# Grouped-query heads: the mean square of each query from TensorE transposes and ScalarE row sums

## The chip, the core and the metric

The kernel runs on one core of a Trainium2 chip. A core has TensorE (PE in the profile, with its weight loads as PEld), VectorE (DVE), ScalarE (ACT), GpSimd (POOL), a queue of its own for transfers (SP), and two on-chip memories: SBUF, and PSUM, which has eight banks and to which TensorE writes its results. Each engine takes its instructions strictly in the order in which the built program lists them, and waits at one until the semaphores that it names have been reached. The metric is the device time of one execution in microseconds (us).

## The reference, cut to what matters

The program is one step of a backbone with two trunk layers and a SwiGLU feed-forward after each. The second layer attends with eight query heads over two key heads, and each query is RMS-normed over its 128 features before it is rotated:

```python
q = rms_norm(q.reshape(b, L, GQA_HEADS, GQA_HEAD_DIM), q_norm)   # x * rsqrt(mean(x*x) + eps) * g
...
q = apply_rope(q, cos, sin)
...
s = jnp.einsum('bqkgd,bskd->bkgqs', qi, k) * scale
p = jax.nn.softmax(s, axis=-1)
```

There are 640 tokens: 512 latent tokens and 128 prompt tokens, in five blocks of 128. The factor rsqrt(mean(q*q) + eps) is one number for each query token, so it can be left out of q and multiplied into the scores of that token's row, inside the exponential of the softmax. Both kernels do that.

## The kernel before, in words

Activations lie with features on the 128 partitions and tokens along the free dimension. Every product is taken in three passes of a split operand (a high part, and a low part that holds the rest): high by high, high by low, low by high. The change touches the grouped-query layer alone.

**A head's queries.** `gqa_q(h)` makes eight pieces, q0 to q7. Pieces q0 to q3 are 24 matmuls that accumulate the first half of the tokens (320 columns) in one bank of PSUM, called `gq`; q4 to q7 do the second half in another. At the end of a half, `done` (L1824) copies the bank to SBUF on ScalarE (L1825, tile `gqc`), squares it on ScalarE (L1826, `gsq`), rotates it on VectorE (`rope`, L1729 to L1732, tile `gqr`) and splits it in high and low (`gqh` on ScalarE, L1829; `gql` on VectorE, L1830).

**The row factor.** `rstd` (L1833) multiplies the squares, as the stationary operand, with two columns of ones: five matmuls in full fp32, each of which the profile records twice, put the sum of squares of each token on that token's partition (tile `gr`). ScalarE turns the five columns into exp(-0.5 ln(mean + eps)), tile `rq` (L1837, L1838).

**Scores and softmax.** `gqa_scores` makes pieces s0 to s4, one for each block of 128 queries. Six matmuls write a score tile `gs` of 128 queries by 640 keys (s4, the prompt: 128 by 128) into one of two pairs of banks. VectorE takes the row maximum (`gn`, L1854), multiplies it with `rq` (`gb`, L1864), and ScalarE writes the exponential with its row sum (`gp`, L1865); an ACTIVATION_READ_ACCUMULATOR that follows fetches the sum. GpSimd divides by the sum (L393). For the first block this second half stands in the order as a piece of its own, x0, behind r.

**Values.** `values` transposes the weights, four 128x128 transposes a block (pieces t0 to t4, tile `gt`), splits them in `gts_h` on ScalarE (L401) and `gts_l` on VectorE (L402), and multiplies them with the values (pieces v0 to v4, tile `go`; the prompt's are pt, pv, `gtp`, `gop`). `oG` (L1893, L1894) is the head's output in SBUF.

**The order.** The loop at the end runs one pass for each head h. A pass has the scores of head h, the queries of head h + 1 and the values of head h - 1, and issues them to TensorE in the order of the string `GQA_ORDER`. The order of the other engines is chosen by a scheduler when the program is built.

**Banks.** Tiles `gq`, `gr`, `gt`, `go`, `gtp` and `gop` come from one pool, `psp`, tag "m", of four banks. A new tile takes a bank that an earlier one has given up, and its first matmul waits for the last reader of that earlier tile. `go` holds its bank from v0 to the end of v4. The score pairs take the four other banks (tag "s", two pairs).

**SBUF.** Tag "t" has three tiles of 128x640, tag "u" seven of 128x320.

Of the kernel before, what the change touches and what calls it, by code (L numbers as in the profile page):

```python
# [11 lines left out]
F32 = mybir.dt.float32  # L12
F32R = mybir.dt.float32r
AF = mybir.ActivationFunctionType
# [4 lines left out]
P = 128  # L19
# [5 lines left out]
HT = T // 2  # L25
# [26 lines left out]
def body(ctx, tc, xT, vecs, crow, wm0, wm0g1, wm0g, wm1, wA, wNV, wNA, wMK, wMV, wOA, wGQ, wGK, wGV, wOC,  # L52
# [3 lines left out]
    V, S, G = nc.vector, nc.scalar, nc.gpsimd  # L56
# [18 lines left out]
    tp = ctx.enter_context(tc.tile_pool(name="tp", bufs=4))  # L75
# [5 lines left out]
    def open_y(**tags):  # L81
        if ypool:
            ypool["stack"].close()
        ypool["stack"] = ExitStack()
        ypool["n"] = ypool.get("n", 0) + 1
        ypool["pool"] = ypool["stack"].enter_context(tc.tile_pool(name=f"psy{ypool['n']}", bufs=1, space=PSUM))
        ypool["tags"] = tags

    def bank(name, kind="m"):
        if kind == "m":  # L90
            return psp.tile([P, 512], F32, tag="m", bufs=4, name=name)
        return ypool["pool"].tile([P, 512], F32, tag=kind, bufs=ypool["tags"][kind], name=name)
# [10 lines left out]
    def tmp(name):  # L103
        return tp.tile([P, T], F32, tag="t", bufs=3, name=name)

    def f(ap):
        return ap.bitcast(F32)
# [7 lines left out]
    def run(pieces):  # L115

        for piece in pieces:
            with tc.issue_after(PE.last.ins):
                piece()

    def sequence(order, pieces):

        left = dict(pieces)
        run([left.pop(name) for name in order.split() if name in left])
        assert not left, list(left)

    def named(prefix, pieces):
        return {f"{prefix}{i}": piece for i, piece in enumerate(pieces)}
# [6 lines left out]
    ones = main.tile([P, P], F32, name="ones")  # L135
    V.memset(ones, 1.0)
    eps = main.tile([P, 1], F32, name="eps")
# [11 lines left out]
    def vcol(i):  # L149
        return vec[:, i:i + 1]  # L150
# [17 lines left out]
    def unit(src, n, name, lo="v", pool=None, bufs=3):  # L168

        raw = load(src, n, name + "r")  # L170
        t = (pool or wp).tile([P, 2, 1024], F32R, tag="w", bufs=bufs, name=name)
        hi, lw = t[:, 0, :n], t[:, 1, :n]
        S.activation(hi, raw, AF.Copy)
        (V if lo == "v" else G).tensor_tensor(lw, raw, f(hi), ALU.subtract)
        return hi, lw

    def after(inst, fn):
        if inst is None:
            return fn()
        with tc.issue_after(inst.ins):  # L180
            return fn()
# [223 lines left out]
    def tr(out, in_):  # L405
        PE.transpose(out, in_, ident)
# [72 lines left out]
    def pieces_of(ps_name, bk, whl, hh, hl, ks, c0, c1, done, w0=0, step=2):  # L479

        box = {}

        def piece(j0, j1):
            def run():
                if j0 == 0:
                    box["ps"] = bk(ps_name)
                wh, wl = whl()
                proj(box["ps"], wh, wl, hh, hl, ks[j0:j1], c0, c1, first=j0 == 0, last=j1 == len(ks), w0=w0 + j0)
                if j1 == len(ks):
                    done(box["ps"])  # L490
            return run
        return [piece(j, min(j + step, len(ks))) for j in range(0, len(ks), step)]
# [4 lines left out]
    def lazy(fn):  # L497
        box = []

        def get():  # L500
            if not box:
                box.append(fn())
            return box[0]
        return get
# [128 lines left out]
    for kk in range(4):  # L633
# [3 lines left out]
        for j in range(2):  # L637
            k = 2 * kk + j
            a, b = wh[:, 512 * j:512 * (j + 1)], wl[:, 512 * j:512 * (j + 1)]
            for i in range(5):  # L640
                c0, c1 = P * i, P * i + P
# [264 lines left out]
    for h in range(8):  # L906
        p, r = divmod(h, 2)
# [9 lines left out]
        pieces = named("s", sc)  # L917
# [60 lines left out]
    def mla_scores(h, pts, beside):  # L978
        r = h % 2
        ll = tiny.tile([P, 4], F32, tag="ll", bufs=4, name=f"ml{h}")  # L980

        def piece(j):
            qh, ql = mqs[h]
            pss = bank2(f"ms{h}_{j}")
            kh, kl = [t[0] for t in k_tiles(r, h // 2)]
            scores(pss, (qh[:, P * j:P * j + P], ql[:, P * j:P * j + P]), kh, kl)
            if j in beside:
                beside[j](pss[:, :, HT:HT + P])
            nm = tiny.tile([P, 1], F32, tag="nm", name=f"mn{h}_{j}")
            V.tensor_reduce(nm, pss[:, :, :HT], AX.XY, ALU.max, negate=True)  # L990
            pt = cp.tile([P, T], F32, tag="mp", bufs=8, name=f"mp{h}_{j}")
            exps[h, j] = S.activation(halves(pt), pss[:, :, :HT], AF.Exp, bias=nm, accum_out=ll[:, j:j + 1])
            softmax_tail(pt, ll[:, j:j + 1], f"mr{h}_{j}", T)
            pts.append(pt)
        return [lambda j=j: piece(j) for j in range(4)]
# [36 lines left out]
    for h in range(8):  # L1032
        p, r = divmod(h, 2)
# [7 lines left out]
        pieces = named("s", mla_scores(h, pts, beside))  # L1041
# [676 lines left out]
    gp = sb.enter_context(tc.tile_pool(name="gp", bufs=1, reuse_waits="tile"))  # L1718
# [6 lines left out]
    def rope(dst, src, gcol, c, name):  # L1725

        c0, c1 = HALF[c]
        b = tp.tile([P, HT], F32, tag="u", bufs=7, name=name + "b")
        V.scalar_tensor_tensor(dst, src, gcol, tg[:, 0, c0:c1], ALU.mult, ALU.mult)  # L1729
        V.scalar_tensor_tensor(b[0:64], src[64:128], gcol[64:128], tg[64:128, 1, c0:c1], ALU.mult, ALU.mult)  # L1730
        V.scalar_tensor_tensor(b[64:128], src[0:64], gcol[0:64], tg[0:64, 1, c0:c1], ALU.mult, ALU.mult)
        V.tensor_tensor(dst, dst, b, ALU.add)  # L1732
# [81 lines left out]
    def gqa_q(h):  # L1814
        get = lazy(lambda: after(gqs[h - 1][3][0] if h > 1 else None, lambda: unit(wGQ[h], 1024, f"wgq{h}", lo="v" if h == 1 else "v")))
        qh = gp.tile([P, T], F32R, tag="gqh", bufs=2, name=f"gqh{h}")
        ql = gp.tile([P, T], F32R, tag="gql", bufs=2, name=f"gql{h}")
        rq = tiny.tile([P, 5], F32, tag="rq", bufs=2, name=f"rq{h}")
        sq = tmp(f"gsq{h}")
        gqs[h] = qh, ql, rq, []  # L1820
        out = []
        for c, (c0, c1) in enumerate(HALF):
            def done(ps, c=c, c0=c0, c1=c1):
                qc = tp.tile([P, HT], F32, tag="u", bufs=7, name=f"gqc{h}{c}")  # L1824
                gqs[h][3].append(S.activation(qc, ps[:, :HT], AF.Copy))  # L1825
                S.activation(sq[:, c0:c1], qc, AF.Square)  # L1826
                qr = tp.tile([P, HT], F32, tag="u", bufs=7, name=f"gqr{h}{c}")
                rope(qr, qc, vcol(V_GQ), c, f"gqr{h}{c}")
                S.activation(qh[:, c0:c1], qr, AF.Copy)  # L1829
                V.tensor_tensor(ql[:, c0:c1], qr, f(qh[:, c0:c1]), ALU.subtract)  # L1830
            out += pieces_of(f"gq{h}{c}", qbank, get, hh, hl, list(range(KT)), c0, c1, done)

        def rstd():  # L1833
            pr = bank(f"gr{h}")
            for j in range(5):
                PE.matmul(pr[:, 2 * j:2 * j + 2], sq[:, P * j:P * j + P], ones[:, 0:2], start=True, stop=True)
            S.activation(rq, pr[:, 0:10].rearrange("p (a b) -> p a b", b=2)[:, :, 0], AF.Ln, bias=eps, scale=1.0 / P)  # L1837
            S.activation(rq, rq, AF.Exp, bias=lnsc, scale=-0.5)  # L1838
        return out + [rstd]

    def gqa_scores(h, pts):
        v = h // 4
# [52 lines left out]
        return {"pt": prompt_t, "pv": prompt, **t}  # L1895

    open_y(s=2)
    *qp, rstd = gqa_q(0)
    run(qp)
    tail, oG = {}, []  # L1900
    GQA_ORDER = "s0 r x0 t0 q0 s1 t1 q1 t2 s2 q2 v0 t3 s3 q3 v1 t4 s4 pt q4 v2 q5 q6 v3 q7 v4 pv"
    for h in range(8):
        oG.append(gp.tile([P, T], F32, tag="go", bufs=8, name=f"oG{h}"))
        pts = []
        pieces = gqa_scores(h, pts)
        pieces["r"] = rstd
        if h < 7:
            *qp, rstd = gqa_q(h + 1)
            pieces.update(named("q", qp))
        sequence(GQA_ORDER, {**pieces, **tail})  # L1910
        tail = gqa_values(h, pts, oG[h])
# [181 lines left out]
```

## Time and profile before

| | before |
|---|---|
| runs | 1477.95 us median of 3 (1476.01 to 1478.81) |
| profiled execution: span from first to last instruction | 1475.7 us |
| PE busy | 1440.4 us, 98% |
| DVE busy | 1235.6 us, 84% |
| ACT busy | 783.4 us, 53% |
| POOL busy | 176.0 us, 12% |
| the grouped-query heads | about 847 to 997 us of the span |

The page gives no time of the profiled execution as a whole beside its span, so the span stands for it: it lies 2.25 us under the median of the runs and 0.3 us under the fastest. How to read the rows: an instruction's row has its start, its duration, its engine, its line, and output<-input. In the rows by stretch, each engine has its busy time and (in brackets) its number of instructions, and PEclk is the granted share of TensorE's clock. Matmuls are pipelined, so the recorded 0.31 us of a 128x320 matmul is longer than the step from one to the next. The rows on which the prediction rests are shown in it.

### The profile page before, as it was taken

How to read it: one execution, taken by the hardware profiler on the slowest of the kernel's cores; microseconds unless marked ns; L12 is line 12 of the kernel's file. 1: busy time of each engine (PE TensorE's matmuls, PEld its weight loads, DVE VectorE, ACT ScalarE, POOL GpSimd, SP SyncE). 2: the span in 40 equal slices, each digit the busy share in tenths (PEclk: the TensorE clock that was granted, in tenths of full speed). 3: DMA queues.
4: the chain of work that ended last, by engine and by line, in shares of the span. 5: the costliest groups of instructions: out<-in, count | busy, mean ns of one | idle time of the engine just before them, and what ended most of it. 6: DMA issues, size and time to landing. Idle time of an engine off the chain costs nothing.

```text
span 1475.7 us, 25826 instructions
## 1 busy us (share of the span) xinstructions
PE 1440.4 (98%) x9764; PEld 1390.5 (94%) x9764; DVE 1235.6 (84%) x2391; ACT 783.4 (53%) x1539; POOL 176.0 (12%) x270
## 2 busy tenths in 40 slices
PE   5999999999999999999999999999999999999997
PEld 3989978889999999999999999989999999999997
DVE  5877788877998889965997878888899898989976
ACT  5446677853755545531223656672656555555443
POOL 0046635420000000000000122220000000000000
PEclk9999999999999999999999999999999999999999
DMA  9643431025164555568764300115245555548572
GB/s 374 217 153 125 144 115 44 15 90 182 48 214 164 169 167 173 183 232 315 240 224 143 100 30 30 43 39 190 86 167 181 182 175 184 176 145 297 181 267 72
DMA packets 79637, 231.49 MB, mean 157 GB/s; under 512 B 8856, under 2 KB 13240, under 8 KB 79128
## 3 DMA queue, kind: packets, MB, share of 16 engines
q1 hardware_dynamic: 77152, 225.43, 44.8%
q10 hardware_dynamic: 1944, 3.48, 0.7%
q8 instruction: 76, 1.25, 0.3%
q0 software_dynamic: 416, 0.93, 0.2%
q14 instruction: 49, 0.40, 0.1%
HBM read 193.15 MB, written 36.66 MB: 156 GB/s over the span
## 4 chain that ended last, share of the span: by engine, by line
PE 75%; DVE 11%; DMA 5%; ACT 5%; issue 3%; POOL 1%; DVEq 0%; ACTq 0%; SPq 0%; POOLq 0%
PE fg L64 14%; PE fd L64 6%; PE fgo L64 5%; PE fo L64 5%; PE gq L64 4%; PE fu L64 3%; PE fdo L64 2%; PE gs L64 2%; PE go L64 2%; PE nq L64 2%; PE nk L64 1%; PE fuo L64 1%; DVE junk L1660 1%; PE gt L68 1%; DMA wm<-in_wm 1%
## 5 line engine op out<-in xcount | busy, mean ns | idle before, releaser
L1660 DVE SCALAR_TENSOR_TENSOR junk<-wm,cb 128x1024 bf16<-128x1024 f32 x88 | 107.3, 1220 | 6.7 <-DMA wm<-in_wm 5.5
L64 PE MATMUL gq<-h10h,wgq 128*128 128x320 f32 x256 | 66.3, 318 | 0.0
L267 POOL TENSOR_SCALAR h10h<-h10t,gs,mods 128x320 fp32r<-128x320 f32 x4 | 4.0, 992 | 430.8 <-DVE h10t L261 428.5
L1400 ACT ACTIVATE wY<-s 128x1024 fp32r<-128x1024 f32 x38 | 40.3, 1061 | 25.7 <-PE fg L64 21.1
L1928 POOL TENSOR_TENSOR xr<-xw,fn1rs 128x320 f32<-128x320 f32 x2 | 1.7, 858 | 412.9 <-ACT fn1rs L235 412.9
L1400 ACT ACTIVATE wZ<-s 128x1024 fp32r<-128x1024 f32 x38 | 40.1, 1055 | 15.4 <-PE fd L64 10.3
L1401 DVE TENSOR_TENSOR wZ<-s,wZ 128x1024 fp32r<-128x1024 f32 x38 | 46.3, 1220 | 1.4
L1401 DVE TENSOR_TENSOR wY<-s,wY 128x1024 fp32r<-128x1024 f32 x38 | 46.3, 1219 | 0.3
L64 PEld LDWEIGHTS gq<-h10h,wgq 128*128 128x128 f32 x256 | 45.3, 190 | 0.6
L1509 DVE TENSOR_TENSOR sg<-up,sg 128x640 f32<-128x640 f32 x38 | 31.3, 823 | 15.8 <-ACT sg L1508 14.8
L1508 ACT ACTIVATE sg<-fg 128x320 f32<-128x320 f32 x38 | 16.7, 439 | 48.4 <-PE fg L64 48.4
L64 PE MATMUL gq<-h10l,wgq 128*128 128x320 f32 x128 | 39.8, 311 | 0.0
L1530 ACT ACTIVATE p<-fd 128x320 f32<-128x320 f32 x38 | 16.6, 438 | 42.5 <-PE fd L64 42.5
L1865 ACT ACTIVATE gp<-gs,gb,rq 128x640 f32<-128x640 f32 (+1 forms) x40 | 31.8, 796 | 13.4 <-DVE gb L1864 12.0
L64 PE MATMUL fg<-h01E,wW 128*128 128x320 f32 x228 | 36.6, 309 | 1.1 <-DVE g L1540 1.1
L64 PE MATMUL fg<-h01N,wZ 128*128 128x320 f32 x228 | 36.6, 309 | 0.3 <-ACT p L1528 0.3
L64 PE MATMUL fg<-h01C,wY 128*128 128x320 f32 x228 | 36.6, 309 | 0.2 <-ACT u L1534 0.2
L64 PE MATMUL fg<-h11N,wZ 128*128 128x320 f32 x228 | 36.7, 309 | 0.0
L64 PE MATMUL fg<-h01q,wX 128*128 128x320 f32 x228 | 36.7, 309 | 0.0
L64 PE MATMUL fu<-h11q,wX 128*128 128x320 f32 x228 | 36.6, 309 | 0.0
L64 PE MATMUL fd<-h11q,wZ 128*128 128x320 f32 x228 | 36.6, 309 | 0.0
L64 PE MATMUL fd<-h01q,wZ 128*128 128x320 f32 x228 | 36.5, 309 | 0.0
(3421 smaller groups left out, 5313.5 us busy)
## 6 DMA issues: line engine op xcount, KB each, us to landing
wm<-in_wm SPq DMA_DIRECT2D x48, 512.0 KB, 4.3
mraw<-in_wm SPq DMA_DIRECT2D x8, 1024.0 KB, 13.2
mraw<-in_wm SPq DMA_DIRECT2D x14, 512.0 KB, 3.7
wmv<-in_wm0g SPq DMA_DIRECT2D x8, 512.0 KB, 4.0
wm<-in_wm0g SPq DMA_DIRECT2D x8, 512.0 KB, 5.4
ruo<-in_wFO SPq DMA_DIRECT2D x8, 512.0 KB, 4.1
rgo<-in_wFO SPq DMA_DIRECT2D x8, 512.0 KB, 5.5
x<-in_xT SPq DMA_DIRECT2D x8, 320.0 KB, 5.2
```

Source lines behind the costliest of these rows:

```text
L64: cls.last = nc.tensor.matmul(*a, **k)
L68: cls.last = nc.tensor.transpose(*a, **k)
L267: G.tensor_scalar(h[:, c0:c1], t, self.gsl[:, k, 0:1], self.ml[:, self.sh + k, 0:1], ALU.mult, ALU.add)
L1400: S.activation(h, src, AF.Copy)
L1401: V.tensor_tensor(w_, src, f(h), ALU.subtract)
L1508: last = S.activation(sg[:, 0:HT], g[:, :HT], AF.Silu, scale=-1.0)
L1509: V.tensor_tensor(sg, up, sg, ALU.mult)
L1530: S.activation(p5, b5[:, :HT], AF.Copy)
L1660: V.scalar_tensor_tensor(junk, raw, 1.0, cb[:, c, :], ALU.mult, ALU.mult, accum_out=mods[l][:, j0 + i, c:c + 1])
L1865: gexp[h, j] = S.activation(dst, src, AF.Exp, bias=nb, scale=rq[:, j:j + 1], accum_out=ll[:, j:j + 1])
L1928: G.tensor_tensor(x[k][:, c0:c1], root[1][k], nrm.rs[:, c0:c1], ALU.mult)
```

## The change

The squares and the products with ones go. The copy of the query bank is now one tile of 128x640 for both halves (`qf`, tag "t", in the place of the squares). TensorE transposes its blocks of 128 tokens into PSUM, and ScalarE reads each transposed block with a Square that also sums along the row, which gives one column of `ss` for each block. Blocks 0 and 1 of head h + 1 are done in a new piece, ra, between t4 and s4 of pass h (tile `gra`, a further tile of tag "m"); blocks 2, 3 and 4 in r (tile `gr`). The two instructions that make `rq` then read `ss` from SBUF.

```diff
-        sq = tmp(f"gsq{h}")
+        qf = tmp(f"gqf{h}")
+        ss = gp.tile([P, 5], F32, tag="ss", bufs=2, name=f"gss{h}")
...
-                qc = tp.tile([P, HT], F32, tag="u", bufs=7, name=f"gqc{h}{c}")
+                qc = qf[:, c0:c1]
                 gqs[h][3].append(S.activation(qc, ps[:, :HT], AF.Copy))
-                S.activation(sq[:, c0:c1], qc, AF.Square)
...
+        def squares(name, blocks):
+            pr = bank(f"{name}{h}")
+            for i, j in enumerate(blocks):
+                tr(pr[:, P * i:P * i + P], qf[:, P * j:P * j + P])
+            for i, j in enumerate(blocks):
+                junk = gp.tile([P, P], F32, tag="sqj", bufs=1, name=f"sqj{h}{j}")
+                S.activation(junk, pr[:, P * i:P * i + P], AF.Square, accum_out=ss[:, j:j + 1])
+
         def rstd():
-            pr = bank(f"gr{h}")
-            for j in range(5):
-                PE.matmul(pr[:, 2 * j:2 * j + 2], sq[:, P * j:P * j + P], ones[:, 0:2], start=True, stop=True)
-            S.activation(rq, pr[:, 0:10].rearrange("p (a b) -> p a b", b=2)[:, :, 0], AF.Ln, bias=eps, scale=1.0 / P)
+            squares("gr", (2, 3, 4))
+            S.activation(rq, ss, AF.Ln, bias=eps, scale=1.0 / P)
             S.activation(rq, rq, AF.Exp, bias=lnsc, scale=-0.5)
-        return out + [rstd]
+        return out + [lambda: squares("gra", (0, 1)), rstd]
...
-    *qp, rstd = gqa_q(0)
-    run(qp)
+    *qp, early, rstd = gqa_q(0)
+    run(qp + [early])
...
-    GQA_ORDER = "s0 r x0 t0 q0 s1 t1 q1 t2 s2 q2 v0 t3 s3 q3 v1 t4 s4 pt q4 v2 q5 q6 v3 q7 v4 pv"
+    GQA_ORDER = "s0 r x0 t0 q0 s1 t1 q1 t2 s2 q2 v0 t3 s3 q3 v1 t4 ra s4 pt q4 v2 q5 q6 v3 q7 v4 pv"
```

How the built order moves is shown at three places of the pass of head 3. Numbers behind a name tell buffers apart; `Activation_49`, `DVE_49`, `PE_49` and `Pool_49` are the progress of ScalarE, VectorE, TensorE and GpSimd.

The first is TensorE from the end of t4 to the first matmul of q4. Before:

```order
L68 MATMUL gt_4_10890<-ident,gp_3_10616 128x128
L64 MATMUL gs_4_10901<-gkh_9589,gqh_10489 128x128 [waits Activation_49]
L64 MATMUL gs_4_10901<-gkl_9591,gqh_10489 128x128
L64 MATMUL gs_4_10901<-gkh_9589,gql_10490 128x128
L68 MATMUL gtp_10912<-ident,gp_4_10661 128x128 [waits Activation_49,Pool_49]
L64 MATMUL gq_10918<-h10h_9448,wgq_10770 128x320 [waits DVE_49,PE_49]
```

The same place now:

```order
L68 MATMUL gt_4_10921<-ident,gp_3_10641 128x128
L68 MATMUL gra_10930<-ident,gqf_10761 128x128 [waits Activation_49]
L68 MATMUL gra_10930<-ident,gqf_10761 128x128
L64 MATMUL gs_4_10939<-gkh_9589,gqh_10509 128x128 [waits PE_49]
L64 MATMUL gs_4_10939<-gkl_9591,gqh_10509 128x128
L64 MATMUL gs_4_10939<-gkh_9589,gql_10510 128x128
L68 MATMUL gtp_10950<-ident,gp_4_10691 128x128 [waits DVE_49,PE_49,Pool_49]
L64 MATMUL gq_10956<-h10h_9448,wgq_10803 128x320 [waits Activation_49]
```

Two transposes have come in, the bank that `gtp` waits for is now one that VectorE frees, and the first matmul of q4 waits for ScalarE where it waited for VectorE.

The second is ScalarE at the same time, from the split of t3's transposes to the prompt's. Before:

```order
L401 ACTIVATE gts_3h<-gt_3_10845 128x512 [waits PE_49,Activation_49]
L1825 ACTIVATE gqc_10876<-gq_10767 128x320 [waits PE_49]
L173 ACTIVATE wgq_11011<-wgq5r 128x1024 [waits DMAHW1_49]
L1865 ACTIVATE gp_3_10857,gl_10729<-gs_3_10856,gb_3_10855,rq_10491 128x640 [waits DVE_49]
L1826 ACTIVATE gsq_10733<-gqc_10876 128x320 [waits Activation_49]
L401 ACTIVATE gts_4h<-gt_4_10890 128x512 [waits PE_49]
L1829 ACTIVATE gqh_10730<-gqr_10879 128x320 [waits DVE_49]
L1865 ACTIVATE gp_4_10902,gl_10729<-gs_4_10901,gb_4_10900,rq_10491 128x128 [waits DVE_49,PE_49]
L401 ACTIVATE gtp2h<-gtp_10912 128x128 [waits PE_49]
```

Now:

```order
L401 ACTIVATE gts_3h<-gt_3_10878 128x512 [waits PE_49]
L1826 ACTIVATE gqf_10761<-gq_10800 128x320 [waits PE_49]
L173 ACTIVATE wgq_11052<-wgq5r 128x1024 [waits DMAHW1_49]
L1871 ACTIVATE gp_3_10890,gl_10757<-gs_3_10889,gb_3_10888,rq_10511 128x640 [waits DVE_49]
L401 ACTIVATE gts_4h<-gt_4_10921 128x512 [waits PE_49,Activation_49]
L1839 ACTIVATE sqj_10933,gss_10762<-gra_10930 128x128 [waits PE_49]
L1839 ACTIVATE sqj_10935,gss_10762<-gra_10930 128x128 [waits Activation_49]
L1829 ACTIVATE gqh_10758<-gqr_10910 128x320 [waits DVE_49]
L401 ACTIVATE gtp2h<-gtp_10950 128x128 [waits PE_49]
L1871 ACTIVATE gp_4_10940,gl_10757<-gs_4_10939,gb_4_10938,rq_10511 128x128 [waits DVE_49,Pool_49]
```

The square of the half is gone, and two squares of transposed blocks stand behind the split of t4's transposes; the second waits for the first.

The third is ScalarE at the start of that pass, from the output of head 1 to the first exponential. Before:

```order
L1893 ACTIVATE oG_10246<-gop_10723 128x128 [waits PE_49]
L1837 ACTIVATE rq_10491<-gr_10745,eps 128x5 [waits PE_49]
L1829 ACTIVATE gqh_10489<-gqr_10711 128x320 [waits DVE_49]
L1838 ACTIVATE rq_10491<-rq_10491,lnsc 128x5 [waits Activation_49]
L401 ACTIVATE gts_0h<-gt_0_10758 128x512 [waits PE_49]
L1865 ACTIVATE gp_0_10737,gl_10729<-gs_0_10736,gb_0_10735,rq_10491 128x640 [waits DVE_49]
```

Now:

```order
L1899 ACTIVATE oG_10258<-gop_10751 128x128 [waits PE_49]
L1829 ACTIVATE gqh_10509<-gqr_10739 128x320 [waits DVE_49]
L1839 ACTIVATE sqj_10778,gss_10513<-gr_10774 128x128 [waits PE_49,Activation_49]
L401 ACTIVATE gts_0h<-gt_0_10791 128x512 [waits PE_49]
L1839 ACTIVATE sqj_10780,gss_10513<-gr_10774 128x128 [waits Activation_49]
L1839 ACTIVATE sqj_10782,gss_10513<-gr_10774 128x128 [waits Activation_49]
L1843 ACTIVATE rq_10511<-gss_10513,eps 128x5 [waits Activation_49]
L1844 ACTIVATE rq_10511<-rq_10511,lnsc 128x5 [waits Activation_49]
L401 ACTIVATE gts_1h<-gt_1_10828 128x512 [waits PE_49]
L1871 ACTIVATE gp_0_10766,gl_10757<-gs_0_10765,gb_0_10764,rq_10511 128x640 [waits DVE_49]
```

Three squares and the split of t1's transposes now stand between the split of the queries and the first exponential.

More of the change, by code (lines that the diff above doesn't have):

```diff
@@ L1907, in body @@
         if h < 7:
-            *qp, rstd = gqa_q(h + 1)
+            *qp, pieces["ra"], rstd = gqa_q(h + 1)
             pieces.update(named("q", qp))
```

## The prediction

> **What bounds the kernel now.** I read the page first, then the rows by stretch over the heads, then the chain of waits there, then the order of time of ScalarE and TensorE in one pass.
>
> ```profile
> span 1475.7 us, 25826 instructions
> PE 1440.4 (98%) x9764; PEld 1390.5 (94%) x9764; DVE 1235.6 (84%) x2391; ACT 783.4 (53%) x1539; POOL 176.0 (12%) x270
> ```
> ```profile
> 866.00:884.00 18.00, 18.00 (x112) 17.18 (x112) 13.31 (x31) 11.02 (x26) 3.74 (x5) 0.91 0.14 45
> 902.00:920.00 18.00, 18.00 (x126) 17.21 (x126) 14.48 (x33) 11.34 (x28) 3.74 (x5) 1.00 0.10 30
> ```
> ```profile
> 902.03 0.93 PE gs L64 x6
> 902.96 1.01 PE gr L64 x10
> 903.97 0.50 PE gt L68 x4
> ...
> 906.22 0.44 PE gt L68 x4
> ...
> 921.03 1.01 PE gr L64 x10
> ```
>
> In the pass of head 3, 902 to 920 us, TensorE is busy for all 18.00 us, ScalarE for 11.34. The chain runs from one TensorE group to the next, and a pass takes 921.03 - 902.96 = 18.07 us. So TensorE sets the time, and what comes off its queue is gained as long as nothing that it waits for comes later than now. The products with ones (`gr`) take 1.01 us, and 0.06 more in the transposes behind them (0.50 against 0.44): 1.07 us. A transpose takes 0.44 / 4 = 0.11 us.
>
> **The change on TensorE.** Five transposes, 0.55 us, for 1.07: 0.52 us less a head. Three stand at r, so what follows r can come 1.07 - 0.33 = 0.74 us earlier; two stand at ra and put what follows there 0.22 later. By this term alone, seven passes that TensorE bounds would win 3.6 us.
>
> **What q4 waits for.** The pool has four banks. When TensorE reaches q4 after the change, it has handed out `go` (held until v4), t4's `gt`, `gra` and `gtp`. There is no fifth, so q4's bank is one that one of these gives up. The order rows say which: before, q4 waited for VectorE (t3's split, a bank that is free by then); now it waits for ScalarE, and of the four only `gra` is read by ScalarE alone. So q4 may start once the second square of `gra` is done, and that stands in ScalarE's queue behind a weight split, an exponential and t4's split. How late is that? The rows of before:
>
> ```profile
> 912.66 0.44 ACT L1825 ACTIVATE gqc<-gq 128x320 f32<-128x320 f32 x1 [0.67 <-PE gq L64]
> 913.00 1.05 ACT L173 ACTIVATE wgq<-wgq5r 128x1024 fp32r<-128x1024 f32 x1
> 913.95 0.88 ACT L1865 ACTIVATE gp<-gs,gb,rq 128x640 f32<-128x640 f32 x1
> 914.71 0.20 ACT L1865 ACTIVATION_READ_ACCUMULATOR gp<-gs,gb,rq 128x1 f32 x1
> 914.81 0.47 ACT L1826 ACTIVATE gsq<-gqc 128x320 f32<-128x320 f32 x1
> 915.17 0.60 ACT L401 ACTIVATE gts_4h<-gt 128x512 fp32r<-128x512 f32 x1
> 915.67 0.47 ACT L1829 ACTIVATE gqh<-gqr 128x320 fp32r<-128x320 f32 x1
> 916.04 0.44 ACT L1865 ACTIVATE gp<-gs,gb,rq 128x128 f32<-128x128 f32 x1
> 916.39 0.19 ACT L1865 ACTIVATION_READ_ACCUMULATOR gp<-gs,gb,rq 128x1 f32 x1
> 916.48 0.26 ACT L401 ACTIVATE gtp2h<-gtp 128x128 fp32r<-128x128 f32 x1
> ```
> ```profile
> 907.73 0.54 PE L64 MATMUL gs<-gkh,gqh 128*128 128x320 f32 x2
> 913.95 0.40 PE L64 MATMUL gq<-h10h,wgq 128*128 128x320 f32 x1
> ```
>
> A square that sums does not occur in the trace. Its nearest rows are the 128x128 copy out of PSUM (0.26) and the 128x128 exponential with its sum (0.44), which also reads a scale and a bias for each partition. Of those two operands one costs about 0.09 us, by exponentials of one size with a bias, and with both:
>
> ```profile
> L992 ACT ACTIVATE mp<-ms,mn 128x640 f32<-128x640 f32 x32 | 25.4, 794 | 9.9 <-DVE mn L990 7.3 <-DVE mr_3r L392 2.2
> L1865 ACT ACTIVATE gp<-gs,gb,rq 128x640 f32<-128x640 f32 x32 | 28.3, 883 | 12.8 <-DVE gb L1864 11.4 <-issue 0.9 <-DVE gr_0r L392 0.4
> ```
>
> A square has neither, so I take 0.44 - 2 x 0.09 = 0.26, and keep 0.44 as the dear end. Its sum is fetched by a read of 0.19 that starts 0.10 before its end: 0.35 us in all. Without `gsq`, t4's split starts at 914.81; the next instruction follows 0.50 later (915.17 to 915.67), at 915.31, and the first square ends at 915.66. The second waits for it (about 0.03) and ends at 916.04. TensorE would be at q4 at 913.95 + 0.22 = 914.17, so it stands still for 1.9 us, and q4 starts 916.05 - 913.95 = 2.1 us later than now, counted from the same copy of q3's bank. At the dear end it is 2.1 + 2 x 0.18 = 2.5. Queued behind q4 are its whole chain (q4 to q7, v2 to v4) and the next head's scores, so all of it is the pass's time. Nothing hides it: TensorE is full.
>
> **What the first exponential waits for.** At the pass's start the saved 0.74 us has to get past s2, whose bank pair waits for x0's exponential.
>
> ```profile
> 901.09 0.44 ACT L1825 ACTIVATE gqc<-gq 128x320 f32<-128x320 f32 x1 [2.41 <-PE gq L64]
> ...
> 904.01 0.27 ACT L1837 ACTIVATE rq<-gr,eps 128x5 f32<-128x5 f32 x1 [1.32 <-PE gr L64]
> ...
> 904.53 0.29 ACT L1838 ACTIVATE rq<-rq,lnsc 128x5 f32<-128x5 f32 x1
> ...
> 905.26 0.89 ACT L1865 ACTIVATE gp<-gs,gb,rq 128x640 f32<-128x640 f32 x1
> 906.05 0.19 ACT L1865 ACTIVATION_READ_ACCUMULATOR gp<-gs,gb,rq 128x1 f32 x1
> ```
> ```profile
> 903.27 0.49 DVE L1732 TENSOR_TENSOR gqr<-gqr,gqr31b 128x320 f32<-128x320 f32 x1
> ```
>
> The rotation ends at 903.76 as now, since it hangs on the copy at 901.09. In the new order ScalarE then has `gqh` (next start 0.37 later, as at 915.67), 904.15; a square to its next start, 0.26, 904.41; t0's split, 0.50, 904.91; two squares, 905.26 and 905.64; the logarithm 905.67 to 905.94, the exponential 905.97 to 906.26; t1's split, next start 906.66; then x0, which ends 0.98 after its start (905.26 to 906.24), 907.64. So s2 starts at about 907.65 against 907.73. The pass keeps 0.1 us of the 0.74 and stands still for the rest. At the dear end three squares add 0.54, and s2 is 0.45 later than now.
>
> So a pass costs 2.1 - 0.1 = 2.0 us more (2.5 + 0.45 = 2.95 at the dear end), and this holds for the six passes 1 to 6, which have both q4 and a predecessor's values: 12.0 us. In pass 5 ScalarE's order also puts a weight split of the output projection (1.05 us, as at 913.00) between the two squares: 1.0 more. Pass 0 has no values; there ra waits for the copy of the bank that q3 has just left, but TensorE stands still later in that pass anyway, and I take 0.5 for two squares less a `gsq`. The last pass has no q4, but its first exponential is late:
>
> ```profile
> 973.36 0.44 ACT L1825 ACTIVATE gqc<-gq 128x320 f32<-128x320 f32 x1 [0.35 <-PE gq L64]
> ```
> ```profile
> 975.60 0.49 DVE L1732 TENSOR_TENSOR gqr<-gqr,gqr71b 128x320 f32<-128x320 f32 x1
> ```
> ```profile
> 978.55 0.56 PE L64 MATMUL gs<-gkh,gqh 128*128 128x320 f32 x2
> 981.06 0.56 PE L64 MATMUL gs<-gkh,gqh 128*128 128x320 f32 x2 [0.23 <-ACT gp L1865]
> 983.59 0.33 PE L64 MATMUL gs<-gkh,gqh 128*128 128x128 f32 x1 [0.26 <-ACT gp L1865]
> ```
>
> From 976.1, the same list with the splits of t1 and t2 ahead of x0 gives x0 at 979.4 to 980.4, against s2 at 978.55: 1.8 later, less the two waits of 0.23 and 0.26 that go: 1.3.
>
> Sum: 12.0 + 1.0 + 0.5 + 1.3 = 14.8 us, on the profile's span 1490.5, on the median 1492.8.
>
> **The clock.** A standstill can cost twice.
>
> ```profile
> 863.27:866.68 3.41, 2.90 (x22) 2.58 (x22) 3.35 (x7) 1.85 (x7) 0.59 (x1) 1.00 0.33 117
> 866.68:870.09 3.41, 3.41 (x15) 3.37 (x14) 2.07 (x6) 2.05 (x5) 0.00 (x0) 0.50 0.09 37
> 303.50:306.90 3.40, 2.34 (x15) 1.91 (x15) 2.89 (x6) 2.44 (x6) 1.54 (x2) 1.00 0.44 154
> 306.90:310.30 3.40, 3.40 (x23) 2.97 (x22) 3.22 (x7) 2.88 (x6) 1.60 (x2) 1.00 0.00 0
> ```
>
> For 3.41 us from 866.68 the granted clock is 0.50, after a stretch with two short waits, the products with ones and transposes; after a standstill of 1.06 us at 303.5 it stays at 1.00. The pass with the half clock has a mean of 0.91 over 18 us: 0.09 x 18 = 1.6 us lost. A standstill of 1.9 us with six transposes just ahead of it lies between what has and what has not brought it. I take it in three of the six passes: 4.8 us, bounds 0 and 9.6.
>
> [...]
>
> **The forecast: 1477.95 + 14.8 + 4.8 = 1497.5 us**, slower by 1.3%.
>
> **The rivals.**
>
> - Full clock throughout: 1492.8, or 1494.4 with one halving. For it speaks 303.5, against it 866.68.
> - Dear squares: six passes at 2.95 give 17.7 for 12.0, and the last pass's three squares 0.54, so 1499.0 at full clock and up to 1508.6 with six halvings. For it speaks only that no such square is in the trace.
> - Faster: ScalarE's new work fits in the idle time that its rows show (0.67 us ahead of 912.66, 2.41 ahead of 901.09), so that the second square of `gra` ends by 914.17, when TensorE comes to q4, and x0 by 907.73 - 0.74 = 906.99. Then TensorE's own account holds: 1477.95 - 3.6 = 1474.3. Against it: the built order has both squares behind t4's split, 1.9 us too late for the one, and x0 0.65 too late for the other.
> - No change: q4's bank is free in time after all (the wait for ScalarE in the order row means an earlier reader), and only x0 is late. A pass then costs 0.22 - 0.1 = 0.1 more, and with pass 0 and the last the sum is 0.7 + 0.5 + 1.3 = 2.5: 1480.5. The count of banks speaks against it.
>
> **How the numbers follow.** Forecast 0.50 (its own range, two to four halvings: 1496 to 1499.2), full clock 0.24, dear squares 0.19, faster 0.04, no change 0.02, something else 0.01. With about 0.2% (3 us) as what a measurement of this kernel can tell, faster 0.04, within 0.02, slower 0.94. The range is 1487 to 1510: below, the full-clock sum less some 40% of its 14.8, should the standstills be shorter than by the rows; above, the dear end with six halvings and 1.4 for what this leaves out.
>
> **What would show it.** Right: a wait of TensorE at `gq` for the square of `gra` (L1839) in six passes, near 1.9 us each; one at `gs` for `gp` near 0.7 at s2; a pass of about 20 us or 21.6 with a halving; transposes of 0.11 where `gr` took 1.07. Wrong: passes of 17.6 us with TensorE full, a square with its read far from 0.35 us, or a loss outside the heads (after 1000 us of the old span), on which none of this rests.

## The result

| | time |
|---|---|
| before | 1476.98 us median (1475.68 to 1478.81, 4 runs) |
| after | 1495.78 us median (1494.08 to 1497.43, 4 runs) |
| after / before | 1.0134, 95% interval 1.0122 to 1.0146 |
| predicted | 1497.5 us, range 1487 to 1510 |

The change makes the kernel slower by 18.8 us, 1.3%. The profiled execution after the change has a span of 1492.3 us and a time of 1494.08 us, so 1.8 us lie around the span.

The page of the changed kernel, three lines of it: the span, the busy times, and the costliest group of its query products, whose idle time before it is now ended by a square:

```profile
span 1492.3 us, 25829 instructions
...
PE 1440.0 (96%) x9724; PEld 1387.7 (93%) x9724; DVE 1233.0 (83%) x2391; ACT 790.9 (53%) x1603; POOL 175.2 (12%) x270
...
L64 PE MATMUL gq<-h10h,wgq 128*128 128x320 f32 x256 | 66.7, 320 | 11.5 <-ACT sqj L1839 8.7
```

TensorE is as busy as before (1440.0 against 1440.4 us) in a span that is 16.6 us longer: it does no more work, it waits.

**What it waits for.** The waits of TensorE in the heads, first in the kernel before and then after the change (us in total, times, longest):

```profile
PE gs L64 <- ACT gp L1865: 0.6, 3, 0.3
```
```profile
PE gq L64 <- ACT sqj L1839: 8.7, 5, 1.8
PE gs L64 <- ACT gp L1871: 6.5, 8, 2.9
PE gq L64 <- DVE gts_4l L402: 2.9, 1, 2.9
```

The first row is the wait of q4 for the second square of `gra`. It is there in five passes; in the sixth, pass 5, q4 has the bank of t4's `gt` and waits for VectorE's part of its split, `gts_4l`. The second is the late first exponential at s2. In the kernel before, all such waits at `gs` came to 0.6 us.

**One pass.** The pass of head 3, as a stretch (its length, then busy time and instructions of PE, PEld, DVE, ACT and POOL, the granted clock, DMA share and GB/s), before and after the change:

```profile
901.87:919.94 18.07, 18.07 (x127) 17.28 (x126) 14.55 (x33) 11.41 (x28) 3.74 (x5) 1.00 0.11 31
```
```profile
904.42:924.72 20.30, 18.10 (x122) 16.87 (x121) 14.15 (x33) 12.36 (x36) 3.75 (x5) 1.00 0.10 27
```

It takes 20.30 us where it took 18.07, with the clock at 1.00 in both. TensorE's records leave 20.30 - 18.10 = 2.20 us of it idle, where before they left none. ScalarE, with 12.36 us of work in it, is far from full. In order of time on ScalarE and then TensorE, around q4:

```profile
915.25 0.44 ACT L1826 ACTIVATE gqf<-gq 128x320 f32<-128x320 f32 x1 [0.74 <-PE gq L64]
915.58 1.05 ACT L173 ACTIVATE wgq<-wgq5r 128x1024 fp32r<-128x1024 f32 x1
...
917.39 0.59 ACT L401 ACTIVATE gts_4h<-gt 128x512 fp32r<-128x512 f32 x1
917.87 0.28 ACT L1839 ACTIVATE sqj<-gra 128x128 f32<-128x128 f32 x1
918.03 0.21 ACT L1839 ACTIVATION_READ_ACCUMULATOR sqj<-gra 128x1 f32 x1
918.27 0.28 ACT L1839 ACTIVATE sqj<-gra 128x128 f32<-128x128 f32 x1
```
```profile
916.68 0.30 PE L68 MATMUL gtp<-ident,gp 128*128 128x128 f32 x1
918.69 0.42 PE L64 MATMUL gq<-h10h,wgq 128*128 128x320 f32 x1 [1.71 <-ACT sqj L1839]
```

The squares of `gra` stand on ScalarE behind a weight split, an exponential (left out above) and t4's split, and the second ends at 918.27 + 0.28 = 918.55. Only then has q4 a bank. From the copy of q3's bank to q4 it is 918.69 - 915.25 = 3.44 us, and it was 913.95 - 912.66 = 1.29.

And around s2:

```profile
903.63 0.44 ACT L1826 ACTIVATE gqf<-gq 128x320 f32<-128x320 f32 x1 [2.63 <-PE gq L64]
...
906.72 0.26 ACT L1839 ACTIVATE sqj<-gr 128x128 f32<-128x128 f32 x1
...
908.25 0.30 ACT L1843 ACTIVATE rq<-gss,eps 128x5 f32<-128x5 f32 x1
...
909.26 0.88 ACT L1871 ACTIVATE gp<-gs,gb,rq 128x640 f32<-128x640 f32 x1
910.03 0.20 ACT L1871 ACTIVATION_READ_ACCUMULATOR gp<-gs,gb,rq 128x1 f32 x1
```
```profile
910.28 0.56 PE L64 MATMUL gs<-gkh,gqh 128*128 128x320 f32 x2 [0.49 <-ACT gp L1871]
```

s2 comes 910.28 - 904.42 = 5.86 us after the pass's start; before it was 907.73 - 901.87 = 5.86. What TensorE saved ahead of s2 it loses there in full.

**Where the 16.6 us of span lie.** The first matmul of head 0's queries and the first of the output projection's `oc0b` bound the heads, in the kernel before and after:

```profile
843.54 0.31 PE L64 MATMUL gq<-h10h,wgq 128*128 128x320 f32 x1
...
996.67 0.31 PE L64 MATMUL oc0b<-oGs0h,ocw 128*128 128x320 f32 x1
```
```profile
841.86 0.31 PE L64 MATMUL gq<-h10h,wgq 128*128 128x320 f32 x1
...
1011.92 0.31 PE L64 MATMUL oc0b<-oGs0h,ocw 128*128 128x320 f32 x1
```

Ahead of the heads the second execution is 1.7 us shorter. I take that for chance, since this point lay between 841.4 and 845.9 us over the profiled executions of this study, of which there is one for each kernel. The heads take 170.06 us for 153.13: 16.9 us more. Behind them the rest takes 480.4 us for 479.0 (span less the start of `oc0b`): 1.35 more. The sum is 16.6.

### The profile page after: what moved, and what is told of

Read it like the earlier page. It is cut to its first block, busy times and chain, and to the rows that moved or that the text cites. A ratio compares the mean times of both kernels' runs of the same rounds, so it can differ in the third digit from the quotient of the medians.

```text
span 1492.3 us, 25829 instructions
## 1 busy us (share of the span) xinstructions
PE 1440.0 (96%) x9724; PEld 1387.7 (93%) x9724; DVE 1233.0 (83%) x2391; ACT 790.9 (53%) x1603; POOL 175.2 (12%) x270
## 4 chain that ended last, share of the span: by engine, by line
PE 83%; DVE 6%; ACT 6%; DMA 2%; issue 2%; DVEq 0%; ACTq 0%
PE fg L64 20%; PE fd L64 9%; PE fgo L64 5%; PE fo L64 5%; PE fu L64 4%; PE gq L64 3%; PE fdo L64 2%; PE nk L64 2%; PE nq L64 2%; PE fuo L64 1%; PE gs L64 1%; PE go L64 1%; DMA mraw<-in_wm 1%; DMA wm<-in_wm 1%; ACT gp L1871 1%
## 5 line engine op out<-in xcount | busy, mean ns | idle before, releaser
L1400 ACT ACTIVATE wZ<-s 128x1024 fp32r<-128x1024 f32 x38 | 40.1, 1056 | 14.8 <-PE fd L64 11.2
L1530 ACT ACTIVATE p<-fd 128x320 f32<-128x320 f32 x38 | 16.6, 437 | 44.3 <-PE fd L64 44.3
L64 PE MATMUL fg<-h11q,wX 128*128 128x320 f32 x228 | 36.6, 309 | 0.0
```

Of the source, the lines that this page charges most:

```text
L64: cls.last = nc.tensor.matmul(*a, **k)
L1400: S.activation(h, src, AF.Copy)
L1530: S.activation(p5, b5[:, :HT], AF.Copy)
```

## The experiments

The theory: q4's wait for the bank of `gra` (1.85 us a pass) and the late first exponential at s2 (0.6) are the loss, and each goes with the place of one piece. The rivals: the five squares cost ScalarE time wherever they stand; the halved clock is most of the loss; the transposes or the new tile cost more than they save. Each ratio below is to runs of the kernel before that were timed beside the experiment (medians of 1476.03 to 1476.46 us), with its 95% interval in brackets. "A halving" is a stretch of 3.41 us in which the granted clock is 0.50 (866.68 to 870.09 in the kernel before, 876.74 to 880.15 after the change).

### The prompt's transpose moved behind q4

```diff
- ... v1 t4 ra s4 pt q4 v2 q5 q6 v3 q7 v4 pv
+ ... v1 t4 ra s4 q4 v2 pt q5 q6 v3 q7 v4 pv
```

> The changed kernel with one piece moved: pt, the prompt's transpose, stands behind v2 instead of ahead of q4, so that q4 is the tile handed out behind gra and takes the bank of t4's gt or an older one. Transposes, squares and their places stay. Theory (q4 stands still 1.85 us for the bank of gra, s2 some 0.6 us for a late x0): the wait at gq for the square goes, the one at gs stays; passes of 20.3 - 1.85 = 18.4 to 18.6 us in place of 20.3, six of them, and 1.1 more from pass 5: 1495.8 - 11 to 12 = about 1484 to 1485.5. Rival (the five squares load ScalarE, 5 x 0.35 us, and a pass pays for them wherever TensorE meets them): the wait only changes its name, passes stay at 20 and the time above 1492. Rival (clock): without the standstill of 1.85 us the granted clock would stay at 1.00 in the heads, and that alone would give 2 to 3.5 us: 1492 to 1494.

Measured: 1483.54 us, ratio to before 1.005 (1.0033 to 1.0066). No transpose or square moved, only the tile that asks for a bank just ahead of q4. Its waits in the heads and a little behind them:

```profile
PE gs L64 <- ACT gp L1871: 6.5, 8, 2.9
PE gtp L68 <- ACT sqj L1839: 1.7, 5, 0.4
PE gtp L68 <- POOL gp L393: 1.4, 1, 1.4
```

The wait at `gq` for the square is gone and that at `gs` is what it was. A little of it came back: `gtp` now waits 0.3 to 0.4 us for the same squares, and once, in pass 5, 1.4 us for GpSimd's division of the weights that it transposes. The pass of head 3 takes 18.82 us, 1.5 less, and the kernel 12.2 us less than after the change. Not all of that is the bank: this execution has no halving in the heads, and the one after the change has two, worth some 2.7 us (1.5 and 1.2, see below); the mean granted clocks are 0.997 and 0.995. But passes at full clock are 1.5 us shorter too, so the count of banks was the cause of the larger part. A load of ScalarE was not, since that has not changed (12.37 us of work in the pass, against 12.36).

### All five blocks in r

```diff
+            squares("gra", (0, 1))
             squares("gr", (2, 3, 4))
...
-        return out + [lambda: squares("gra", (0, 1)), rstd]
+        return out + [rstd]
...
- ... v1 t4 ra s4 pt q4 ...
+ ... v1 t4 s4 pt q4 ...
```

> All five transposes and squares in r, in two banks; ra and its bank are gone. Theory: q4 no longer waits for a square (1.85 us a pass gone, pass 5's 1.1 too); two more squares (2 x 0.35) stand ahead of x0, so that the wait at s2 grows from 0.6 by 0.7 less the 0.22 that the two transposes take there: about 1.1 us. A pass then takes 20.3 - 1.85 - 0.22 + 0.7 = 18.9 us, and the time is 1495.8 - 6 x 1.4 - 1.1 + 1 (pass 0 and last) = about 1487. Rival (ScalarE's load decides): still 5 squares a head, so no change, 1493 to 1497. Rival (x0's lateness decides, not q4): slower than 1495.8.

Measured: 1487.07 us, ratio 1.0077 (1.0062 to 1.0092). The expected 1487, and the expected trade:

```profile
PE gs L64 <- ACT gp L1872: 11.8, 8, 3.8
```
```profile
891.42 0.56 PE L64 MATMUL gs<-gkh,gqh 128*128 128x320 f32 x2 [1.07 <-ACT gp L1872]
```

No wait is left at `gq`; the one at s2 has grown from 0.49 to 1.07 us with two more squares ahead of the first exponential. A pass takes 18.88 us. That this is faster than the split into an early and a late part shows that the early part cost more than it won.

### The squares left out

```diff
-        ss = gp.tile([P, 5], F32, tag="ss", bufs=2, name=f"gss{h}")
+        ss = ones[:, 0:5]
...
-            for i, j in enumerate(blocks):
-                junk = gp.tile([P, P], F32, tag="sqj", bufs=1, name=f"sqj{h}{j}")
-                S.activation(junk, pr[:, P * i:P * i + P], AF.Square, accum_out=ss[:, j:j + 1])
```

> The transposes stay where they are, the squares are left out and the row factor comes from a constant, so the queries are not normed. Theory: with nobody to read gra and gr neither wait is left, and TensorE's own account shows: 0.52 us less a head than before, passes of 18.07 - 0.5 = 17.6 us with TensorE full, 1477.0 - 3.6 = 1473.4 (1472 to 1475). Rival (the transposes themselves cost more than the products that they replace, or the new tile for the copy does): passes at or above 18.07, 1477 or more. Rival (a halved clock behind six transposes in a row): a halving in the heads although TensorE is full.

Measured: 1472.58 us, ratio 0.998 (0.9971 to 0.999).

```profile
881.18:898.74 17.56, 17.56 (x121) 16.76 (x121) 13.78 (x32) 10.48 (x25) 3.67 (x5) 1.00 0.08 30
```

With every transpose in its place and nobody reading them, this pass, that of head 2, is full of TensorE work and takes 17.56 us, 0.51 under the 18.07 of before. (The others took 17.7 to 18.4, with short pauses.) So TensorE's own account is what the prediction said, and the loss is in the waits for the squares, not in the transposes. Passes 3 to 5, of 17.91 to 17.94 us, leave TensorE idle for 0.13 to 0.14 us each (17.91 - 17.77 in pass 3); I put that down to the new tile, behind which `gtp` has the bank of t3's `gt`, an estimate that no row here shows. No halving came in passes 1 to 6: the granted clock is 1.00 from 863.45 to 970.92 us, with six transposes in a row in each pass, t4's four and the two of ra (891.75 and 892.19 in pass 2).

### r ahead of s0

```diff
- s0 r x0 t0 q0 ...
+ r s0 x0 t0 q0 ...
```

> The changed kernel with r moved ahead of s0: the transposes of blocks 2, 3 and 4 need only the copy of the second half, which is done some 0.5 us before TensorE gets there, and their squares can run on ScalarE while the rotation is still on VectorE. ra stays. Theory: the wait at s2 (0.6 us) goes and the one at q4 (1.85) stays; passes of 20.3 - 0.6 = 19.7 us, seven heads, 1495.8 - 4 to 5 = about 1491.5. Rival (the wait at s2 hangs on the rotation or on t0's split, not on the squares): s2 waits as before, 1495 to 1497. Rival (the transposes now wait for the copy): each pass longer by up to 0.4, 1498.

Measured: 1490.69 us, ratio 1.0099 (1.0077 to 1.0121).

```profile
PE gq L64 <- ACT sqj L1839: 6.9, 4, 1.7
PE gq L64 <- DVE gts_4l L402: 4.9, 2, 3.3
PE gs L64 <- ACT gp L1871: 1.7, 2, 1.5
```

The wait at s2 is gone from the six middle passes (what is left of it is in the first and the last), and a pass without a halving takes 19.52 us for 20.3. q4's wait is as it was in passes 1 to 4 (1.71 to 1.72 us for the square); in passes 5 and 6 it is for VectorE's split of t4's `gt`, 3.3 and 1.5 us. The two waits are separate: the one at s2 went, and the one at q4 stayed. Its four runs lie 7.3 us apart (1487.09 to 1494.40), with mean granted clocks of 0.996, 0.995, 0.993 and 0.989 in the same order. That is the widest spread of any kernel here, and it follows the clock.

### ra behind q5

```diff
- ... v1 t4 ra s4 pt q4 v2 q5 q6 v3 ...
+ ... v1 t4 s4 pt q4 v2 q5 ra q6 v3 ...
```

> The changed kernel with ra, the two early transposes and their squares, behind q5 and v2 instead of ahead of s4; nothing else. Theory (q4 waits only because gra takes the fourth bank just ahead of it): q4's wait goes as with pt moved, and the 0.35 us that gtp still waited there go too; s2's wait of 0.6 stays. Passes of 18.8 - 0.35 = about 18.4 us, 1483.5 - 6 x 0.35 = about 1481.5 (1480 to 1483), still above before's 1476.2. Rival (wherever gra stands it costs the bank that comes next: here the prompt's gop, or r's): a wait at gop or gr of 0.5 us or more in each pass and 1484 or more. Rival (s2's lateness goes with the place of the squares): 1477.

Measured: 1482.33 us, ratio 1.0031 (1.0019 to 1.0043); 1.2 us under the first experiment. From pass 2 on the wait that `gtp` had there is gone, and no other has come in its place:

```profile
PE gs L64 <- ACT gp L1871: 6.7, 8, 2.9
```

What stays is the wait at s2. From pass 2 to pass 6 a pass takes 18.3 us; in pass 1 `gra` waited once, for 1.4 us.

### Both moves

```diff
- s0 r x0 t0 ... v1 t4 ra s4 pt q4 v2 q5 q6 v3 ...
+ r s0 x0 t0 ... v1 t4 s4 pt q4 v2 q5 ra q6 v3 ...
```

> Both moves: ra behind q5 and v2, and r ahead of s0. Theory: the wait at q4 and the one at s2 are both gone with all five squares done, so TensorE's own account is left as without squares: passes of 17.6 to 17.9 us against 18.07, 1472.6 to 1475, which is 1 to 4 us under before's 1476.2; and the 1.8 us that were lost behind the heads, in the waits for the split output weights (L174), do not occur, since they were absent in both kernels whose first exponential was not late (r ahead of s0, and no squares). Rival (the two terms overlap, and the second gain is smaller than each alone showed, 10.5 and 5 us): 1478 to 1482. Rival (the squares' own ScalarE time, absent in the run without squares, comes back on another wait): 1477 or more.

Measured: 1475.37 us, ratio 0.9988 (0.9978 to 0.9998). The two gains add up, and the sign turns, though by little. A pass takes 17.95 us, not 17.5, for a new wait:

```profile
896.93 0.41 PE L68 MATMUL gra<-ident,gqf 128*128 128x128 f32 x2 [0.25 <-DVE gts_4l L402]
```

`gra` is now itself the tile that asks for a bank too early, that of t4's `gt`, whose low part VectorE has not split yet.

### The order alone

```diff
- (kernel before)  s0 r x0 t0 q0 ...
+                  r s0 x0 t0 q0 ...
```

> The kernel before, with squares and products with ones, and only its r moved ahead of s0: the control for the order of the pieces. Theory: TensorE was full in the passes before, so the order alone wins nothing there: passes of 18.07 us and 1475.5 to 1477.5. Rival (what the kernel with both moves wins is the order's, not the transposes'): 1473 to 1474.5. Rival (the products with ones now wait for the square of the second half, which ScalarE does after the copy, 0.4 us later): up to 0.4 us a head, 1479.

Measured: 1478.58 us, ratio 1.0011 (1.0002 to 1.002). The order by itself wins nothing; it loses some 0.1%. The products with ones now wait for the square of the second half in three of the passes:

```profile
PE gr L64 <- ACT gsq L1826: 2.4, 3, 1.3
```

In the profiled execution the heads take 153.35 us against 153.13, although they have no halving and those of the kernel before have one (mean granted clocks of 0.998 and 0.996). So what the kernel with both moves wins is due to the transposes, once they stand in the right places.

### ra behind q6

```diff
- ... v2 q5 ra q6 v3 ...
+ ... v2 q5 q6 ra v3 ...
```

> The kernel with both moves, and ra one piece further back, behind q6. With ra behind q5 its first transpose stood still 0.26 to 0.41 us in passes 2 to 5, for the bank of t4's gt, whose low part VectorE had not split yet (gts_4l ends at 896.79, ra came to TensorE at 896.5). Theory: one piece of 0.9 us later the bank is free, the wait goes, and passes are 17.6 us in place of 17.95: 1475.4 - 4 x 0.35 = about 1474 (1473 to 1475), 2 us under before's 1476.5. Rival (the 0.35 us come back at s2, because the squares of ra now reach ScalarE beside the copy of the second half): passes stay at 17.9 and 1475.4.

Measured: 1472.57 us, ratio 0.9978 (0.9969 to 0.9987): 0.22% or 3.2 us faster than before, and as fast as the kernel without squares (1472.58; ratio 0.998).

```profile
902.72:920.23 17.51, 17.51 (x123) 16.73 (x121) 13.79 (x33) 12.40 (x36) 3.74 (x5) 1.00 0.10 33
```

All five squares are done (ScalarE has the same 12.4 us of work in a pass as after the change), TensorE is full in this pass, and it is 0.56 us shorter than before. (The wait that went was 0.25 us in the row shown under "Both moves"; the 0.41 of the expectation is that row's duration.) The clock doesn't explain the win: the mean granted clock was 0.997 over these 11 runs, and 0.997 over the 16 of the kernel before beside them. This is the best version of the study, and the rival by which ScalarE's load decides has fallen with it.

## Why the prediction was right, step by step

- **TensorE's account**, 0.52 us less a head: right. 18.07 - 17.56 = 0.51 without squares and 18.07 - 17.51 = 0.56 in the last kernel.
- **q4 waits for the second square of `gra`**, 1.9 us of standstill and q4 2.1 later: right. q4 started 2.01 us after the transpose ahead of it (918.69 - 916.68), of which 0.11 is the transpose's own place: 1.9 us. (The row's own wait, 1.71, is shorter: it counts from the end of the transpose's recorded 0.30 us, 0.19 more than the 0.11.) It came 3.44 - 1.29 = 2.15 later, counted from the same copy. The first experiment shows that it is the bank, and in the built program q4's `gq` has the bank of `gra` in the five passes in which it waits for the square.
- **A square with its read**, 0.35 us: about right. The group of those of `gra`:

```profile
L1839 ACT ACTIVATE sqj<-gra x16: 258/277/284, 849.4 to 980.4; 128x128 f32<-128x128 f32 x16
L1839 ACT ACTIVATION_READ_ACCUMULATOR sqj<-gra x16: 193/206/219, 849.6 to 980.6; 128x1 f32 x16
```

  The first of pass 3 takes 918.03 + 0.21 - 917.87 = 0.37 us with its read, and the second starts 918.27 - 917.87 = 0.40 us after it (reckoned: 0.35 + 0.03). The dear end (0.53) is refuted.
- **s2 keeps 0.1 us of the 0.74 saved**: it keeps none (5.86 us after the pass's start, in both). The step's list of ScalarE's work ahead of x0 was right in its order; from the copy of the second half to the end of x0 with its read it reckoned 6.55 us, and the rows give 910.03 + 0.20 - 903.63 = 6.60.
- **2.0 us for each of six passes**: by the starts of s0, 2.2 to 2.4 in passes 2, 3, 4 and 6, 1.6 in pass 1, which has one halving in both executions, and 3.3 in pass 5, 1.1 more than in the others (predicted 1.0). There the size was right and the cause was not: the weight split does stand between the two squares, but q4 has the bank of t4's `gt`, whose `gts_4l` is late. q4 starts there at 960.39, before the second square has ended (960.15 + 0.26 = 960.41). Pass 0 lost 0.46 (0.5). The last pass lost 2.5 with a halving in it. In the first experiment, where s2 stands still as long (2.9 us at most, in both) and no halving came, it lost 1.4 (1.3 predicted), so the halving cost about 1.2. The row of pass 5 and the standstill of the last pass:

```profile
960.39 0.41 PE L64 MATMUL gq<-h10h,wgq 128*128 128x320 f32 x1 [2.85 <-DVE gts_4l L402]
...
993.30 0.90 PE L64 MATMUL gs<-gkh,gqh 128*128 128x320 f32 x2 [2.85 <-ACT gp L1871]
```

  All together, the heads lost 16.9 us, and 15.7 without that halving: the sum said 14.8.
- **The clock**, 4.8 us: mis-sized. The profiled execution has two halvings in the heads after the change and one before. The one in pass 1 is in both (from one r to the next, pass 1 takes 884.73 - 865.09 = 19.64 us before, with the halving, and pass 2 takes 18.07 without; after the change they take 21.69 and 20.27; so one costs about 1.5), and the net is the 1.2 of the last pass; the forecast took three of 1.6. No standstill of q4 in passes 2 to 6 was followed by one. Over all runs it may be more: the mean granted clock was 0.9945 in the four runs after the change, and 0.9965 in the 13 runs of the kernel before timed with the first experiment, and 0.002 of 1494 us is 3 us, an estimate. The bounds of 0 and 9.6 hold both.
- **Nothing behind the heads**: wrong, and named as a sign of error. Some 1.4 us were lost there, by waits that the kernel before doesn't have:

```profile
PE oc3a L64 <- DVE ocw L174: 0.5, 1, 0.5
PE oc5a L64 <- DVE ocw L174: 0.4, 1, 0.4
PE oc6a L64 <- DVE ocw L174: 0.3, 1, 0.3
```

  The order in which VectorE works there was built anew. Before, and then after the change:

```profile
1013.68 1.22 DVE L174 TENSOR_TENSOR ocw<-ocw3r,ocw 128x1024 fp32r<-128x1024 f32 x1
...
1015.21 0.67 DVE L333 SCALAR_TENSOR_TENSOR xr<-oc2b,mods,xr 128x192 f32<-128x192 f32 x2
```
```profile
1030.16 0.68 DVE L333 SCALAR_TENSOR_TENSOR xr<-oc2b,mods,xr 128x192 f32<-128x192 f32 x2 [0.29 <-PE oc2b L64]
1030.75 1.22 DVE L174 TENSOR_TENSOR ocw<-ocw3r,ocw 128x1024 fp32r<-128x1024 f32 x1
```

  The split of the weight `ocw3` has slipped behind the two adds of `oc2b`: it starts 18.8 us after the first `oc0b` and not 17.0. The kernels that do the squares with r behind s0 (after the change, and the first, second and fifth experiment) have this order and the waits, and take 480.0 to 480.4 us from `oc0b` to the end of the span; the kernel before and the other five have neither, and take 478.3 to 479.0. That a change in the heads moves the scheduler's order behind them is shown; by which of its costs is not.

So the forecast of 1497.5 came within 1.7 us of the measured 1495.78 partly by luck, because misses offset each other. By the profiled executions it had 3.6 us too much for the clock, 0.9 too little for the heads at full clock and 1.35 too little for what lies behind them; the median of the kernel before also came out 1.0 lower with a fourth run. The mechanism and the size of its main term held.

## What to carry to other kernels

Here an extra tile in a PSUM pool of four banks was paid for by the tile that asked for a bank next, and the price was the place of its last reader in that reader's queue, not the reader's duration: q4 stood still for 1.71 us by its row, for a square of 0.28. So count the pool's tiles at each request, in order, before a piece is split off. And a piece that saved TensorE time did not win where what its results gate came no earlier: s2 came 5.86 us after the pass's start in both kernels, and the saving turned into a wait of 0.49 us there. With both moves and ra behind q6 the pass took 17.51 us for 18.07. When a change loses, move its pieces one at a time: here the same operations in other places went from 1.3% slower to 0.2% faster.

## What the runs showed of the hardware

The same standstill was followed by a halving in some places and not in others. After the change the granted clock is 0.50 in the heads from 876.74 to 880.15 and from 992.79 to 996.20 us: 3.41 us each, with 112.64 between them. In the experiment with r ahead of s0 it goes to 0.50 at 916.18 and at 936.66, 20.48 us apart. With 112.64 taken as 33 steps, one step is 3.413 us, and 20.48 is six of them: an estimate from these times alone. In stretches of the changed kernel counted in such steps from the changes, the same standstill at q4, 1.71 us in the rows, fell into one stretch (873.33) or across two (893.81 and 897.22):

```profile
873.33:876.74 3.41, 1.70 (x14) 1.37 (x13) 3.16 (x8) 3.21 (x9) 0.00 (x0) 1.00 0.00 0
876.74:880.15 3.41, 3.41 (x12) 3.13 (x13) 1.79 (x6) 0.80 (x3) 0.96 (x1) 0.50 0.52 154
893.81:897.22 3.41, 2.88 (x21) 2.51 (x19) 3.25 (x8) 2.70 (x6) 0.80 (x1) 1.00 0.01 2
897.22:900.63 3.41, 2.23 (x13) 2.09 (x14) 3.07 (x8) 1.91 (x8) 0.96 (x1) 1.00 0.18 66
900.63:904.04 3.41, 3.41 (x22) 3.17 (x21) 0.42 (x2) 0.78 (x3) 0.37 (x1) 1.00 0.23 90
```

After the stretch with TensorE busy for 1.70 of 3.41 us, the clock was 0.50; after those with 2.88 and 2.23 it was 1.00. In the experiment with r ahead of s0 a stretch with 1.69 us was followed by 0.50, and one with 1.70 was not:

```profile
892.28:895.69 3.41, 1.70 (x14) 1.37 (x12) 3.35 (x7) 3.26 (x9) 0.49 (x1) 1.00 0.00 0
895.69:899.10 3.41, 3.41 (x22) 3.27 (x23) 2.63 (x9) 1.30 (x4) 1.07 (x2) 1.00 0.47 150
912.76:916.17 3.41, 1.69 (x14) 1.50 (x13) 3.35 (x8) 2.36 (x9) 0.38 (x1) 1.00 0.01 2
916.18:919.59 3.41, 3.41 (x13) 3.12 (x12) 1.75 (x6) 1.12 (x4) 0.94 (x2) 0.50 0.42 154
```

So a stretch with TensorE busy for half of it was followed by a halving in some cases and not in others; in the changed kernel the stretches at 958.66 and 979.14, with TensorE busy for 1.68 and 1.73 us, were followed by a clock of 1.00 too. q4's standstill fell across two stretches in passes 2 to 4 of the changed kernel, with no halving behind it. And in the kernel before, a stretch with TensorE busy for 2.90 us, that of 863.27 in the prediction, was followed by 0.50. What decides stays open. This is why the forecast's "three of six passes" could only be a guess: the heads' start moved by 4.07 us between the profiled executions after the change and of the last kernel (841.86 and 845.93), which is more than the step.
